# Summing the passing weight quarters on two engines instead of loading them: a Strassen-like matmul on one core

## The chip, the cores and the metric

The kernel runs on one core of a Trainium2 chip. The metric is device time in microseconds, the median of several runs. A core has a matrix engine (TensorE, PE in the profile, with PEld for its loading of stationary operands), three engines for elementwise work (VectorE, DVE; ScalarE, ACT; GpSimd, POOL) and SyncE (SP), which here only issues DMA transfers. Operands lie in SBUF, matmul results in the eight banks of PSUM.

## The reference

```python
B, S, D = 8, 2048, 2048
x = randn(B, S, D)   # float32
w = randn(D, D)      # float32

def reference(x, w):
    cs = np.cumsum(x, axis=1)
    diff = cs - shifted(cs)      # zeros ahead of the first row
    return np.matmul(diff, w)
```

The difference of the running sum is x again, so what is computed is x @ w: 16384 rows by 2048 by 2048, in float32 at the ends. The kernel works with 16-bit operands and scales.

## The kernel before, in words

**Rows.** x is cut into 128 row tiles of 128 rows. The first four (PLAIN = 4) are multiplied plainly in bf16 while the weights arrive. The rest are taken four at a time, tiles g, h = g + 2, g + 1 and h + 1, in 31 groups. The first group is `group_plain`; all others are `group`, and from g = 16 on they take its branch `five` (28 groups).

**Products.** Each group is a block product with fewer multiplications than the plain one: halves of rows and of weights are summed beforehand (S1 to S4 for rows, T1 to T4 for weights), and several of the seven inner products are themselves split once more into seven quarter products. A `product` is 16 matmuls, `steps` are the same in four portions (`go` issues the next), a `quarter` is four matmuls of 128x128 by 128x512 into one bank (L531). In a group of the branch `five` TensorE has 208 matmuls in an order written out by hand. The banks of the quarter products are called q, e, v, w; X and Y are pairs of banks of the larger products.

**Weight quarters.** An `Inner` holds the quarters of one weight half that has been split again: t11, t12, t21, t22 and the sums Q1, Q2, Q3 and Q4 = t21 - Q2 (`fourth`). There are four of them: in_2, in_3, in_4, in_5. Only in_3 has a Q4 of its own place, and in_3.t21 is not kept in place: its place was given to other sums. The four quarters without a place "pass": they use in turn one tile of 128x2048 fp16 in SBUF, `flow` (`passed` is its four parts). Each was written once to DRAM (`keep_flow`, and four transfers for in_3.t21) and is brought back by `bring_flow(i)`, a transfer of 512 KB on SyncE's queue. In a group of the branch `five`, flow holds in turn

- in_2.Q4, for the quarter product `quarter(q, a22, Q.Q4, False)` with Q = in_2 (brought by `bring_flow(0)` at the end of the group before),
- in_3.t21, for `quarter(v, b12, passed, False)` (`bring_flow(3)`),
- in_5.Q4, for `quarter(e, a22, passed, True)` (`bring_flow(1)`),
- in_4.Q4, for `quarter(Y[0], a22, Q.Q4, False)` with Q = in_4 (`bring_flow(2)`).

**Results.** `add` (L542) is a DVE instruction that multiplies a bank by the row tile's unit u and adds it to a running sum C in SBUF; `keep` (L539) is a ScalarE instruction that starts such a sum. `put` sends a finished sum to the output by a DMA on SyncE's queue.

**Row tiles on their way in.** For each tile of a later group, `load` issues two transfers into F on SyncE's queue, `weigh` (L112, ScalarE) takes sums of absolute values of both halves, `scale_of` (L129 to L132, three small DVE instructions) makes m, the scale s = 1/m and the unit u = m x uw, `narrow` (L143, ScalarE) writes the scaled halves as fp16, and `turn` (L156) transposes them by two DMA transfers on SyncE's queue. In `group` the tiles on their way are next_g, next_h, next_k, next_l and `then`.

**Order.** The function `after` chains the instructions of each engine in the order in which the program asks for them, so every engine runs its list in exactly that order, and an instruction that waits holds up all behind it on its engine. This holds for SyncE's queue of transfers too. GpSimd's queue has almost nothing: a reduction over partitions and seven output transfers at the start.

Of the kernel before, what the change touches and what calls it, by code (L numbers as in the profile page):

```python
# [10 lines left out]
def kernel(  # L11
# [6 lines left out]
    nc = tc.nc  # L18
# [12 lines left out]
    ADD = mybir.AluOpType.add  # L31
    SUB = mybir.AluOpType.subtract
    MUL = mybir.AluOpType.mult
# [25 lines left out]
    uw = const.tile([P, 1], f32, name="uw")  # L59
# [16 lines left out]
    def after(engine, ask):  # L76
        if engine in last:
            with tc.issue_after(last[engine].ins):
                said = ask()
        else:  # L80
            said = ask()
        last[engine] = said[-1] if isinstance(said, tuple) else said
        return said
# [37 lines left out]
    def scale_of(t):  # L121
        if t < END:
            m2 = sums_of.pop(t)
            m = small.tile([P, 1], f32, name="m1")
            s = scales[t] = small.tile([P, 1], f32, name="s")
            u = unit[t] = units.tile([P, 1], f32, name="u")
            after(
                "dve",
                lambda: nc.vector.tensor_scalar(m, m2[:, :1], m2[:, 1:], TINY, ADD, MAX),  # L129
            )  # L130
            after("dve", lambda: nc.vector.reciprocal(s, m))  # L131
            after("dve", lambda: nc.vector.tensor_scalar(u, m, uw, None, MUL))  # L132

    def narrowed(t):
        return where[t][0].bitcast(f16)

    def narrow(t, sides=range(2)):
        if t < END:
            s = scales[t]
            for i in sides:  # L140
                after(
                    "act",
                    lambda: nc.scalar.activation(  # L143
                        narrowed(t)[:, ds(i * NH, NH)], where[t][i], COPY, scale=s
                    ),
                )
# [14 lines left out]
    with tc.tile_pool(name="ring", bufs=7) as ring, tc.tile_pool(  # L161
# [97 lines left out]
        def put(c, rows, columns, queue=nc.gpsimd):  # L259
            return queue.dma_start(out2[rows, columns], c)  # L260
# [203 lines left out]
    def one_c():  # L464
        return free.pop(0)
# [23 lines left out]
    passed = [flow[:, k, :] for k in range(4)]  # L489
# [4 lines left out]
    def bring_flow(i):  # L494
        after("sp", lambda: nc.sync.dma_start(flow, spill[i]))

    def less(dst, p, q):
        for k in range(len(dst)):
            after("dve", lambda: nc.vector.tensor_tensor(dst[k], p[k], q[k], SUB))  # L499

    def total(dst, p, q, op):
        after("dve", lambda: nc.vector.tensor_tensor(dst.all, p.all, q.all, op))  # L502

# [24 lines left out]
    def quarter(to, a, b, first):  # L528
        def some():
            for k in range(4):  # L530
                said = nc.tensor.matmul(  # L531
                    to, a[k], b[k], start=(first and k == 0), stop=(k == 3), skip_group_check=True
                )
            return said

        after("pe", some)

    def keep(c, p, u):
        after("act", lambda: nc.scalar.activation(c, p, COPY, scale=u))  # L539

    def add(c, p, u):
        after("dve", lambda: nc.vector.scalar_tensor_tensor(c, p, u, c, MUL, ADD))  # L542
# [5 lines left out]
    def adds(c, p, u):  # L548
        for n in range(2):
            add(c[n], p[n], u)  # L550
# [29 lines left out]
    in_2, in_3 = Inner(B21), Inner(B22)  # L580
    in_3.Q4 = [spare.pop() for _ in range(4)]
    in_4, in_5 = Inner(T4), Inner(T1)
# [113 lines left out]
    def group(g, X, Y, q, e, v, w):  # L696
        h = g + 2
        five = g > PLAIN + 8
# [7 lines left out]
        next_g, next_h, next_k, next_l, then = g + 4, h + 4, g + 5, h + 5, g + 8  # L706
# [3 lines left out]
        def go(some, n=1):  # L710
            for _ in range(n):
                next(some)()
# [72 lines left out]
        quarter(q, a22, Q.Q4, False)  # L785
        add(C11h[0], q, uh)
        put(C11h[0], h, 0)
        if five:
            bring_flow(3)
        total(S4h, A12h, S2h, SUB)  # L790
        one, two, A5 = sums_in(
            S1g, S1h, (*passing[:2], S1h.half(0), passing[3])
# [16 lines left out]
        if five:  # L809
            one()  # L810
            two()
            a11, a12, a22, s1, s2, s3, s4 = A5
            b11, b12, b22, r1, r2, r3, r4 = A3
            N, R = in_5, in_3
            go(P7g)
            quarter(v, a12, N.t21, True)
            C22g, C22h = [one_c()], []
            keep(C22g[0], v, vg)
            quarter(q, a11, N.t11, True)
            one4()  # L820
            add(C22g[0], q, vg)
            add(C12g[0], q, ug)
            weigh(next_k)
            go(P7g)
            quarter(w, b11, R.t11, True)
            add(C12g[0], w, ug)
            quarter(v, b12, passed, False)
            bring_flow(1)
            add(C12g[0], v, ug)
            put(C12g[0], g, 2)  # L830
            turn(next_g, [1])
            go(P7g)
            quarter(e, s1, N.Q1, True)
            C22g += [one_c()]
            C22h = [None, one_c()]
            keep(C22g[1], e, vg)
            keep(C22h[1], e, vh)
            go(P7g)
            two4()
            scale_of(next_k)  # L840
            add(C22g[0], X[0], vg)
            put(C22g[0], g + 1, 2)
            narrow(next_k)
            quarter(q, s2, N.Q2, False)
            add(C22g[1], q, vg)
            add(C12g[1], q, ug)
            quarter(w, r2, R.Q2, False)
            add(C12g[1], w, ug)
            add(C22g[1], X[1], vg)
            go(P7h)  # L850
            quarter(e, r1, R.Q1, False)
            add(C12g[1], e, ug)
            add(C12h[1], e, uh)
            turn(next_k, [0])
            turn(next_h, [0])
            load(next_l, 0)
            go(P7h)
            quarter(v, s4, N.t22, True)
            add(C22g[1], v, vg)
            put(C22g[1], g + 1, 3)  # L860
            load(then, 1)
            quarter(q, s3, N.Q3, False)
            C22h[0] = one_c()
            keep(C22h[0], q, vh)
            add(C22h[1], q, vh)
            add(C12h[1], q, uh)
            go(P7h)
            quarter(e, a22, passed, True)
            bring_flow(2)
            add(C22h[0], e, vh)  # L870
            add(C12h[0], q, uh)
            weigh(next_l)
            quarter(v, r4, R.t22, False)
            add(C12g[1], v, ug)
            put(C12g[1], g, 3)
            go(P7h)
            adds(C22h, Y, vh)
            puts(C22h, h + 1, 1)
            scale_of(next_l)
            quarter(e, b22, R.Q4, False)  # L880
            add(C12h[0], e, uh)
            quarter(w, r3, R.Q3, False)
            add(C12h[0], w, uh)
            put(C12h[0], h, 2)
            add(C12h[1], w, uh)
            put(C12h[1], h, 3)
        else:
            if g == PLAIN + 4:
                in_4.first()
            one()  # L890
            two()
            weigh(next_k)
            seven(A3, in_3, C12g, C12h, P7g)
            turn(next_g, [1])
            turn(next_h, [0])
            scale_of(next_k)
            narrow(next_k)
            if g == PLAIN + 4:
                in_4.fourth()
                keep_flow(2)  # L900
                for k in range(4):
                    after("sp", lambda: nc.sync.dma_start(spill[3][:, k, :], in_3.t21[k]))
                in_4.third()
            else:
                in_5.first()
                in_5.fourth()
                keep_flow(1)
            product((v, w), S1g, T1, True)
            C22g = pair()
            keeps(C22g, (v, w), vg)  # L910
            adds(C12g, (v, w), ug)
            puts(C12g, g, 1)
            load(next_l, 0)
            product((q, e), S1h, T1, True)
            C22h = pair()
            keeps(C22h, (q, e), vh)
            adds(C12h, (q, e), uh)
            puts(C12h, h, 1)
            if g > PLAIN + 4:
                bring_flow(2)  # L920
            go(P7g, 2)
            one4()
            two4()
            turn(next_k, [0])
            adds(C22g, X, vg)
            puts(C22g, g + 1, 1)
            go(P7h, 4)
            adds(C22h, Y, vh)
            puts(C22h, h + 1, 1)
            weigh(next_l)  # L930
            scale_of(next_l)
            load(then, 1)
# [7 lines left out]
        quarter(X[0], a12, Q.t21, False)  # L940
        add(C21g[0], X[0], vg)
        put(C21g[0], g + 1, 0)
        narrow(next_l, [0])
        quarter(e, s1, Q.Q1, True)
        C21h = [None, one_c()]
        keep(C21g[1], e, vg)
        keep(C21h[1], e, vh)
        narrow(next_l, [1])
        quarter(X[1], s4, Q.t22, False)
        turn(next_k, [1])  # L950
        turn(next_l, [0])
# [12 lines left out]
        add(C21h[0], q, vh)  # L964
        put(C21h[0], h + 1, 0)
        if next_g < END:
            bring_flow(0)
        turn(next_l, [1])
        if g == PLAIN + 8:
            in_5.third()  # L970
# [37 lines left out]
```

## Time and profile before

| what | value |
|---|---|
| median of 3 runs | 1531.41 us (1529.73 to 1533.57) |
| the profiled execution | 1542.59 us |
| span of the profiled execution | 1540.8 us |
| granted TensorE clock | 0.996 |
| busy: PE, DVE, ACT, POOL | 1487.4, 1228.7, 912.2, 5.1 us |
| HBM read, written | 210.76 MB, 136.31 MB |
| period of a group of the branch five | 46.06 us |

In the profile, lines such as L542 refer to the program above. A group of instructions is written as tile written <- tiles read. A span is one execution from the first to the last instruction; "idle before" is time in which an engine stood still ahead of an instruction, and the name behind the arrow is what it seems to have waited for. Starts are counted from the start of the span. Matmuls are pipelined: one of 128x512 takes 0.38 us from start to end, while the next starts 0.216 us after it; adds and sums on DVE overlap in the same way to a smaller degree.

### The profile page before, as it was taken

How to read it: one execution, taken by the hardware profiler on the slowest of the kernel's cores; microseconds unless marked ns; L12 is line 12 of the kernel's file. 1: busy time of each engine (PE TensorE's matmuls, PEld its weight loads, DVE VectorE, ACT ScalarE, POOL GpSimd, SP SyncE). 2: the span in 40 equal slices, each digit the busy share in tenths (PEclk: the TensorE clock that was granted, in tenths of full speed). 3: DMA queues.
4: the chain of work that ended last, by engine and by line, in shares of the span. 5: the costliest groups of instructions: out<-in, count | busy, mean ns of one | idle time of the engine just before them, and what ended most of it. 6: DMA issues, size and time to landing. Idle time of an engine off the chain costs nothing.

```text
span 1540.8 us, 20681 instructions
## 1 busy us (share of the span) xinstructions
PE 1487.4 (97%) x6793; PEld 662.5 (43%) x6799; DVE 1228.7 (80%) x2315; ACT 912.2 (59%) x1301; POOL 5.1 (0%) x12
## 2 busy tenths in 40 slices
PE   8988999999999999999999999999999999999998
PEld 3433444444444444444444444444444444444443
DVE  7986777787887778888788877878887788778877
ACT  5866555555656546656556656556656556656542
POOL 0100000000000000000000000000000000000000
PEclk9999999999999999999999999999999999999999
DMA  9988989999999999999999999999999999999984
GB/s 362 354 217 249 225 228 279 280 281 242 278 271 273 281 272 255 283 267 281 276 280 251 292 260 277 272 270 273 283 269 279 277 270 255 280 261 288 274 226 143
DMA packets 395179, 413.49 MB, mean 268 GB/s; under 512 B 276736, under 2 KB 277248, under 8 KB 394944
## 3 DMA queue, kind: packets, MB, share of 16 engines
q1 hardware_dynamic: 394512, 410.35, 95.1%
q0 software_dynamic: 560, 1.84, 0.3%
q8 instruction: 53, 0.87, 0.2%
q14 instruction: 54, 0.44, 0.1%
HBM read 210.76 MB, written 136.31 MB: 225 GB/s over the span
## 4 chain that ended last, share of the span: by engine, by line
PE 56%; DMA 21%; DVE 11%; issue 4%; ACT 4%; SPq 2%; DVEq 0%; ACTq 0%
PE b L531 27%; PE b L512 27%; DMA F<-in_x_dram 7%; DMA flow<-spill 6%; DMA x<-F 6%; DVE c L542 5%; PE b L250 2%; DVE x L502 2%; SPq L156 2%; DVE inner L502 2%; DMA out_dram<-c 2%; ACT F L143 1%; ACT waste L112 1%; ACT c L539 1%; DVE W L499 1%
## 5 line engine op out<-in xcount | busy, mean ns | idle before, releaser
L542 DVE SCALAR_TENSOR_TENSOR c<-b,u,c 128x512 f32<-128x512 f32 x1048 | 744.5, 747 | 179.3 <-PE b L531 108.7
L512 PE MATMUL b<-W,x 128*128 128x512 f16 x3072 | 721.3, 381 | 6.0 <-ACT c L539 4.5
L539 ACT ACTIVATE c<-b,u 128x512 f32<-128x512 f32 x496 | 316.1, 681 | 372.2 <-PE b L512 188.8
L512 PEld LDWEIGHTS <-x 128*128 128x128 f16 x3072 | 301.7, 98 | 373.3 <-issue 12.9
L143 ACT ACTIVATE F<-F,s 128x1024 f16<-128x1024 f32 x246 | 282.1, 1147 | 117.3 <-DVE s L131 114.2
L531 PE MATMUL b<-W,inner 128*128 128x512 f16 x1392 | 338.2, 379 | 13.1 <-DVE c L542 13.1
L112 ACT ACTIVATE waste<-F 128x1024 uint8<-128x1024 f32 x246 | 259.5, 1055 | 107.5 <-DMA F<-in_x_dram 103.6
L531 PEld LDWEIGHTS <-inner 128*128 128x128 f16 x1744 | 170.4, 98 | 223.1 <-issue 20.3
L531 PEld LDWEIGHTS <-x 128*128 128x128 f16 x1560 | 150.3, 98 | 218.1 <-issue 26.7
L531 PE MATMUL b<-W,x 128*128 128x512 f16 x968 | 234.4, 379 | 2.1 <-DVE c L542 0.8
L502 DVE TENSOR_TENSOR x<-x,x 128x1024 f16<-128x1024 f16 (+1 forms) x214 | 120.5, 575 | 7.0 <-PE b L512 2.1
L531 PE MATMUL b<-flow,x 128*128 128x512 f16 x352 | 90.6, 380 | 17.9 <-DVE c L542 9.6
L502 DVE TENSOR_TENSOR inner<-x,x 128x1024 f16<-128x1024 f16 (+1 forms) x122 | 67.9, 556 | 24.6 <-DMA x<-F 24.5
L531 PE MATMUL b<-inner 128*128 128x512 f16 x240 | 61.6, 379 | 0.0
L531 PE MATMUL b<-inner,x 128*128 128x512 f16 x240 | 61.6, 379 | 0.0
L250 PE MATMUL b<-wb,xP 128*128 128x512 bf16 x234 | 56.8, 394 | 3.8 <-DVE xP L222 1.6
L502 DVE TENSOR_TENSOR inner<-x 128x512 f16<-128x512 f16 x60 | 25.2, 421 | 37.4 <-PE b L531 35.7
L129 DVE TENSOR_SCALAR m<-m 128x1 f32<-128x1 f32 x124 | 26.0, 209 | 32.9 <-ACT waste L112 32.7
L112 ACT ACTIVATION_READ_ACCUMULATOR waste<-F 128x1 f32 x246 | 46.5, 189 | 0.0
L502 DVE TENSOR_TENSOR x<-inner,x 128x1024 f16<-128x1024 f16 x62 | 42.6, 687 | 3.2
L502 DVE TENSOR_TENSOR inner<-inner 128x512 f16<-128x512 f16 x112 | 42.4, 421 | 1.0
L237 DVE TENSOR_REDUCE wmax<-W 128x1 f32<-128x1024 f32 x32 | 39.0, 1219 | 3.9 <-DMA W<-in_w_dram 2.4
(53 smaller groups left out, 346.4 us busy)
## 6 DMA issues: line engine op xcount, KB each, us to landing
out_dram<-c SPq DMA_DIRECT2D x496, 256.0 KB, 4.1
F<-in_x_dram SPq DMA_DIRECT2D x246, 512.0 KB, 5.2
flow<-spill SPq DMA_DIRECT2D x114, 512.0 KB, 5.6
W<-in_w_dram SPq DMA_DIRECT2D x32, 512.0 KB, 9.3
W<-in_x_dram SPq DMA_DIRECT2D x16, 256.0 KB, 7.2
x<-F SPq DMA_TRANSPOSE x246, 3.9
out_dram<-o SPq DMA_DIRECT2D x7, 256.0 KB, 3.5
spill<-flow SPq DMA_DIRECT2D x3, 512.0 KB, 2.7
```

Source lines behind the costliest of these rows:

```text
L112: lambda: nc.scalar.activation(waste, where[t][i], ABS, scale=1.0 / ROW, accum_out=sums_of[t][:, i : i + 1],),
L129: lambda: nc.vector.tensor_scalar(m, m2[:, :1], m2[:, 1:], TINY, ADD, MAX),
L143: lambda: nc.scalar.activation(narrowed(t)[:, ds(i * NH, NH)], where[t][i], COPY, scale=s),
L156: lambda: nc.sync.dma_start_transpose(place(t)[i], narrowed(t)[:, ds(i * NH, NH)]),
L237: lambda: nc.vector.tensor_reduce(wmax[:, i : i + 1], wt, AX.X, MAX, apply_absolute_value=True),
L250: lambda: nc.tensor.matmul(ps[r][n], xP[:, r, ko, :], wb[h, ko][:, ds(n * NB, NB)], start=(ko == 0), stop=(ko == KO - 1),),
L499: after("dve", lambda: nc.vector.tensor_tensor(dst[k], p[k], q[k], SUB))
L502: after("dve", lambda: nc.vector.tensor_tensor(dst.all, p.all, q.all, op))
L512: said = nc.tensor.matmul(to[n], a[k], b[k][:, n, :], start=(first and k == 0), stop=(k == KH - 1), skip_group_check=True,)
L531: said = nc.tensor.matmul(to, a[k], b[k], start=(first and k == 0), stop=(k == 3), skip_group_check=True)
L539: after("act", lambda: nc.scalar.activation(c, p, COPY, scale=u))
L542: after("dve", lambda: nc.vector.scalar_tensor_tensor(c, p, u, c, MUL, ADD))
```

## The change

No passing quarter is brought from DRAM in the groups of the branch `five`, and in_2.Q4 is not brought in any group. Each is computed again into flow whenever it is needed: in_2.Q4 and in_3.t21 by four DVE sums each (in_3.t21 as in_3.Q4 + in_3.Q2), in_5.Q4 and in_4.Q4 by four GpSimd sums each, in a new function `pass_fourth`. All have 128x512 fp16 operands in SBUF. Of the loads of flow, only `bring_flow(2)` in the group g = 12 remains. The DVE sums for in_3.t21 stand after the sums of rows for in_3, those for in_2.Q4 at the end of the group, each later in program order than the transfer that they replace or in its place. The GpSimd sums stand where the transfers stood.

Besides, u is computed by GpSimd instead of DVE for all row tiles. In the branch `five`, `scale_of(next_l)` moves behind the last three adds of its stretch on DVE, and in every `group` the first half of `narrow(next_l)` moves behind two `keep` on ScalarE, to the second half.

```diff
@@ scale_of
             after("dve", lambda: nc.vector.reciprocal(s, m))
-            after("dve", lambda: nc.vector.tensor_scalar(u, m, uw, None, MUL))
+            after("pool", lambda: nc.gpsimd.tensor_scalar(u, m, uw, None, MUL))
@@ new function
+    def pass_fourth(i):
+        for k in range(4):
+            after("pool", lambda: nc.gpsimd.tensor_tensor(passed[k], i.t21[k], i.Q2[k], SUB))
@@ group
         put(C11h[0], h, 0)
-        if five:
-            bring_flow(3)
         total(S4h, A12h, S2h, SUB)
...
         if five:
             one()
             two()
+            for k in range(4):
+                after('dve', lambda: nc.vector.tensor_tensor(passed[k], in_3.Q4[k], in_3.Q2[k], ADD))
             a11, a12, a22, s1, s2, s3, s4 = A5
...
             quarter(v, b12, passed, False)
-            bring_flow(1)
+            pass_fourth(in_5)
             add(C12g[0], v, ug)
...
             quarter(e, a22, passed, True)
-            bring_flow(2)
+            pass_fourth(in_4)
             add(C22h[0], e, vh)
             add(C12h[0], q, uh)
             weigh(next_l)
...
             puts(C22h, h + 1, 1)
-            scale_of(next_l)
             quarter(e, b22, R.Q4, False)
             add(C12h[0], e, uh)
             quarter(w, r3, R.Q3, False)
             add(C12h[0], w, uh)
             put(C12h[0], h, 2)
             add(C12h[1], w, uh)
             put(C12h[1], h, 3)
+            scale_of(next_l)
...
         put(C21g[0], g + 1, 0)
-        narrow(next_l, [0])
         quarter(e, s1, Q.Q1, True)
         C21h = [None, one_c()]
         keep(C21g[1], e, vg)
         keep(C21h[1], e, vh)
-        narrow(next_l, [1])
+        narrow(next_l)
...
         if next_g < END:
-            bring_flow(0)
+            less(passed, in_2.t21, in_2.Q2)
         turn(next_l, [1])
```

## The prediction, made before the changed kernel had run

> **What bounds the kernel now.** The page came first. TensorE is busy nearly the whole span at a full clock, so only the gaps between its matmuls can be won; the rows say whose they are.
>
> ```profile
> PE 1487.4 (97%) x6793; PEld 662.5 (43%) x6799; DVE 1228.7 (80%) x2315; ACT 912.2 (59%) x1301; POOL 5.1 (0%) x12
> PE 56%; DMA 21%; DVE 11%; issue 4%; ACT 4%; SPq 2%; DVEq 0%; ACTq 0%
> F<-in_x_dram SPq DMA_DIRECT2D x246, 512.0 KB, 5.2
> flow<-spill SPq DMA_DIRECT2D x114, 512.0 KB, 5.6
> x<-F SPq DMA_TRANSPOSE x246, 3.9
> ```
>
> The chain that ended last runs through DMA for 21%. The waits of the steady part, 290 to 1495 us, name the partners:
>
> ```profile
> PEld L531 <- DMA flow<-spill: 19.0, 24, 2.0
> DVE inner L502 <- DMA x<-F: 16.5, 23, 1.5
> PE b L531 <- DVE c L542: 16.4, 28, 1.9
> ```
>
> To size them I read the timeline of TensorE alone. From 655.77 to 662.67 us 32 matmuls start, 0.216 us each; a quarter product (four) takes 0.863. A group of four row tiles has 52 such steps, 44.9 us, and repeats every 46.06. I number the steps 0 to 51 from the group's first product. Wherever a piece starts later than the one before it plus its count times 0.216, the difference is lost time:
>
> ```profile
> 646.68 3.62 PE L531 MATMUL b<-W,x 128*128 128x512 f16 x16
> 651.25 2.75 PE L531 MATMUL b<-W,inner 128*128 128x512 f16 x12 [0.94 <-DVE c L542]
> ...
> 679.08 1.03 PE L531 MATMUL b<-W,x 128*128 128x512 f16 x4
> 680.18 1.04 PE L531 MATMUL b<-flow,x 128*128 128x512 f16 x4
> ```
>
> Step 47 was due at 646.68 + 16 x 0.216 = 650.14 and came at 651.25: 1.11 lost. Step 28 was due at 679.94: 0.24 lost. Added up over 290 to 1495 us (26 groups), the steps that read flow (18 and 28) lose 16.7 us, step 47 loses 16.2, step 51 loses 5.9 (0.21 a time, one running add after step 49; the change leaves it). Little else is lost.
>
> Step 47 rewrites bank e, which DVE must have read. That read stood behind the weighing of the last tile:
>
> ```profile
> 644.15 4.70 DVE L542 SCALAR_TENSOR_TENSOR c<-b,u,c 128x512 f32<-128x512 f32 x7 [0.83 <-ACT c L539]
> 650.01 0.21 DVE L129 TENSOR_SCALAR m<-m 128x1 f32<-128x1 f32 x1 [1.16 <-ACT waste L112]
> 650.26 0.16 DVE L131 RECIPROCAL s<-m 128x1 f32<-128x1 f32 x1
> 650.34 0.20 DVE L132 TENSOR_SCALAR u<-m,uw 128x1 f32<-128x1 f32 x1
> 650.45 2.91 DVE L542 SCALAR_TENSOR_TENSOR c<-b,u,c 128x512 f32<-128x512 f32 x4
> ```
>
> Step 18 is a wait on DVE, which waits for a transpose issued right behind a flow load; step 28 waits for its own flow load. From the chain of waits, 880 to 930 us:
>
> ```profile
> 890.57 8.20 DMA x<-F
> ...
> 901.24 0.67 DVE c L542
> 901.92 0.04 issue
> 901.96 1.04 PE b L531 x4
> ...
> 905.31 6.19 DMA flow<-spill
> 911.50 0.05 issue
> 911.54 1.04 PE b L531 x4
> ```
>
> SyncE issued flow at 890.02 and the transpose at 890.57. It landed after 8.20 us, against a median of 3.9.
>
> **The change part by part.** *Flow loads.* 113 of 114 go (28 groups with three, 29 with the one at the end; one remains at g = 12): 59 of 211 MB read, and three to four issues a group on SyncE's queue, each 0.38 us. Transposes and loads behind them move up. Gained: the 16.7 us of steps 18 and 28, if the new producers are in time.
>
> *Last scale later.* add(C12h[0], e) moves ahead of m, s and u: 1.16 of wait and 0.44 of work leave the way to step 47. The seven adds end at 648.85, e is read by 649.6, before 650.14. Gained: 16.2 us. What is late next: narrow(next_l) now follows three adds (3 x 0.67) and both keeps of e on ScalarE. Its halves end about 0.8 us before and 0.4 after the next group's start, against 4.2 and 1.2 before it now. SyncE reaches these transposes 0.6 before and 4.8 us after that start (655.16, 660.55), so nearly all is covered; without that cover DVE's sum at 667.86 would be late. keep(C21h[0]) on ScalarE slips about 1 us behind the narrowing, and its reader is DVE's last add, reached then anyway.
>
> *Two quarters on DVE.* Eight sums a group; 128x512 f16 sums start 0.335 us apart (658.18, 658.52, 658.85), so 1.34 us for four. The four for in_2 follow the last add (657.8) and push the next seven sums; DVE then sat 2.41 us idle before 663.81, which hides them. The four for in_3 follow the sum at 676.73, end at 678.4 and fill a wait of 1.26 before 678.41; step 28 needs them at 679.94. Zero on the path; without either cover, 1.34 x 28 = 38 us. No queue gets longer than its idle time: DVE gains 2.7 us a group, loses four u (0.11 each), and had over 7 us of waits.
>
> *Two quarters on GpSimd.* No row shows a sum there. Nearest below: the same sum on DVE, 0.42. Nearest above: the slowest work per element, the 128x128 scan on DVE, 0.425, times four: 1.70. I take 1.70, the cautious end, since GpSimd's known rows (memset 128x1, 0.10) say nothing per element. Time allowed: for in_4 from the end of step 40 (645.12) to step 50 (653.83 less the 1.11 lost, plus 0.65 for the fourth matmul), 8.25 us or 2.06 a sum; for in_5 from 680.97 to 690.96, 2.5 a sum. Either bound fits: zero. Behind a waiting sum on that queue stand only u, which are read most of a group later. The u themselves: 0.10 (that memset) to 0.20 (the DVE row), off the path.
>
> *What the two engines do to each other.* No row has both working in SBUF. GpSimd's first batch begins as step 28 ends and meets the two sums of two4:
>
> ```profile
> 682.67 0.41 DVE L502 TENSOR_TENSOR x<-x,x 128x512 f16<-128x512 f16 x1
> 683.00 0.42 DVE L502 TENSOR_TENSOR inner<-x,inner 128x512 f16<-128x512 f16 x1
> ...
> 684.77 5.00 DVE L542 SCALAR_TENSOR_TENSOR c<-b,u,c 128x512 f32<-128x512 f32 x7 [0.26 <-PE b L531]
> ```
>
> DVE has room behind them: waits of 0.26 and 0.83, one u less (0.11), and 0.57 that the read of e then has to spare: 1.8 us. Lower bound of the cost: nothing. If each sum waits for one GpSimd sum of 1.70, two4 ends about 1.6 late: covered. Upper bound: two4 waits for all four sums, 4 x T - 1.46 late, so 4T - 3.26 beyond cover: 3.5 us a group at 1.70. I take 0.1 to 0.2 us a group, 4 us in all, because most margins become thin.
>
> The Trainium skill speaks against this pairing: by its page "SBUF — State Buffer", section "Who interferes with whom", a VectorE instruction with two SBUF inputs and a GpSimd instruction that reads SBUF exclude each other, and the later one blocks for the whole of the other. No row before shows it; by it two4 loses one or two GpSimd sums and the running adds (one input in PSUM) nothing. "GPSIMD Engine Reference", section 3.1, measures 4497 ns for 2048 elements, an estimate of 1.1 us for 512; by that figure both batches end with some 3 us to spare.
>
> **The sum**, against the profiled execution's own 1542.59 us (span 1540.8): 16.7 + 16.2, and some 3 of the 4.6 that the same steps lose between 200 and 290 us (1.61, 2.5, 0.46), less 4: 32 saved, 1510.6. The median of the runs is 1531.41, 11.2 below. If that difference lies elsewhere, 32 come off: 1499. If it lies wholly in these waits, 21: 1510. I take 27: **1504 us**; own range 1494 to 1513.
>
> **Rivals.**
>
> *Held sums (slower).* two4 waits for GpSimd's whole batch. For: the batch starts 1.5 us before two4 in each group. Against: nothing shows that a batch is kept together. It turns the gain into a loss from T = 1.10 on, where 28 x (4T - 3.26) passes 32; at 1.70 it costs 98, net 66: 1597; at 1.2, 43, net 11: 1542. Chance 0.15.
>
> *GpSimd slow (slower).* Over 2.06 us a sum, step 50 waits; at 2.5, 4 x 0.44 x 28 = 49 less 32: 1548. For: nothing about its speed is known from rows. Against: it would be over five times DVE's time. Chance 0.09.
>
> *Transfers stay late.* Landing times hold although flow is gone, because narrow(next_l) comes later; step 18 still waits for DVE. Steps 28 and 47 alone: about 19 saved, 1513 to 1518. For: 16.5 us of DVE waits on transposes. Against: the 8.20 us stood behind a flow load. Chance 0.14.
>
> *Gains and losses cancel*, within 0.3% (about 5 us, what a measurement of this kernel can tell from no change): 1527 to 1536, chance 0.06. That flow traffic would remain has no place: the loads are gone from the queue.
>
> **How the numbers follow.** The main case has 0.56. It and late transfers make it faster by over 0.3%: 0.70, with 0.01 from held sums of a short T: 0.71. Within: 0.06. Slower: 0.23. The range, 1491 to 1537, leaves out a little below and most of the two slower rivals.
>
> **What would show it.** Right: no wait of TensorE on flow at steps 18 and 28 or on DVE at step 47, a period near 45.2 us with 0.21 left at step 51, F loads landing under 5.2 us, GpSimd sums under 2.06. Wrong: steps 37 to 47 waiting for DVE adds while the sums of two4 start after GpSimd's last one; step 50 waiting for GpSimd; or step 18 waiting with its transpose still near 8 us.

## The result, and the profile after

| | before | after |
|---|---|---|
| median, us | 1531.06 (1529.73 to 1533.57, 4 runs) | 1508.07 (1507.42 to 1509.20, 4 runs) |
| ratio, 95% interval | | 0.9849 [0.9832, 0.9866] |
| the profiled execution, us | 1542.59 | 1509.20 |
| span of it, us | 1540.8 | 1507.4 |
| HBM read, MB | 210.76 | 151.52 |
| period of a group of the branch five, us (mean of the last 26) | 46.40 (45.2 to 48.3) | 45.38 (45.37 to 45.39) |

The changed kernel is faster by 23.0 us between the medians and by 33.4 us between the profiled executions. The profiled execution before, 1542.59 us, is not among the four runs of its median and stands 9 us above the slowest of them. The 46.06 us given above as the period before is that of one group, 701.79 to 747.85 us; the mean is 46.40. In later comparisons on two other chips the kernel before took medians of 1541.7 us, on a third 1538.5 with runs from 1531.6 to 1544.9; the changed kernel stayed between 1507.4 and 1511.7 in all its runs. The time of the kernel before moves from chip to chip and from run to run, that of the kernel after hardly does. Side by side on one chip the ratio was 0.9799 [0.9783, 0.9816], 32.2 us.

From the page of the kernel after, its parts 1, 4 and 6 (four lines added to the program move L502 to L506, L512 to L516, L531 to L535, L539 to L543 and L542 to L546):

```profile
PE 1480.5 (98%) x6799; PEld 661.8 (44%) x6799; DVE 1329.6 (88%) x2419; ACT 914.2 (61%) x1301; POOL 328.9 (22%) x360
...
PE 75%; DVE 13%; issue 4%; DMA 4%; ACT 3%; SPq 0%; DVEq 0%; ACTq 0%
...
F<-in_x_dram SPq DMA_DIRECT2D x246, 512.0 KB, 4.9
...
x<-F SPq DMA_TRANSPOSE x246, 3.4
```

DMA had 21% of the chain that ended last and has 4%. Transposes land in 3.4 us instead of 3.9, loads of rows in 4.9 instead of 5.2. DVE's busy share rose from 80% to 88%, more than its 228 new sums of 0.335 us (76 us, 5 points of 1507) explain; the rest is sums that take longer, shown below. From the list of waits of the kernel after, 290 to 1465 us (engine and line, what it waited for, us in total, times, longest):

```profile
POOL flow L503 <- PE b L535: 248.8, 52, 5.1
...
DVE c L546 <- PE b L535: 66.4, 79, 1.1
PEld L535 <- DVE c L546: 14.8, 26, 0.6
...
DVE inner L506 <- DMA x<-F: 0.2, 1, 0.2
```

No wait on flow by TensorE is left, DVE's waits on transposes went from 16.5 to 0.2 us, and one new regular wait has appeared: 26 times, once in each group, TensorE's weight loads wait for a running add. The timeline of TensorE shows where (start, length, operation):

```profile
664.33 1.03 PE L535 MATMUL b<-flow,x 128*128 128x512 f16 x4
...
672.10 1.89 PE L535 MATMUL b<-W,inner 128*128 128x512 f16 x8
673.82 1.03 PE L516 MATMUL b<-W,x 128*128 128x512 f16 x4
674.94 1.04 PE L535 MATMUL b<-flow,inner 128*128 128x512 f16 x4
...
677.57 3.61 PE L535 MATMUL b<-W,x 128*128 128x512 f16 x16
681.01 2.75 PE L535 MATMUL b<-W,inner 128*128 128x512 f16 x12
```

Step 47, 1.11 us late in the group shown before, is on time: due at 677.57 + 16 x 0.216 = 681.03, it came at 681.01.

The product that reads in_5.Q4 was due at 673.82 + 0.863 = 674.68 and came at 674.94. It does not wait for flow: GpSimd had been ready for 5 us. It rewrites bank e and waits for an add that DVE is late with. This is step 40, and it loses 0.24 us in every group. DVE and GpSimd in the same group of the kernel after, from their timelines:

```profile
664.79 4.69 POOL L503 TENSOR_TENSOR flow<-W 128x512 f16<-128x512 f16 x4 [4.43 <-PE b L535]
```

```profile
667.06 1.41 DVE L506 TENSOR_TENSOR x<-x,x 128x512 f16<-128x512 f16 x1
668.39 1.37 DVE L506 TENSOR_TENSOR inner<-x,inner 128x512 f16<-128x512 f16 x1
...
670.00 12.32 DVE L546 SCALAR_TENSOR_TENSOR c<-b,u,c 128x512 f32<-128x512 f32 x18
```

The two sums of two4 (the last sums of rows for in_4) took 0.41 and 0.42 us before; beside GpSimd's batch they take 1.41 and 1.37. After them 18 adds follow without a pause, so DVE has no time left to catch up.

To compare kernels, the lost time of TensorE from 290 us to the end, added up by step from its timeline as in the prediction (us; a dash is nothing over 0.1 at a time):

| kernel | 18 and 28 | 40 | 43 | 47 | 50 | 51 | sum |
|---|---|---|---|---|---|---|---|
| before | 16.7 | - | - | 16.2 | - | 6.1 | 39.1 |
| after | - | 6.3 | - | - | - | 5.8 | 12.1 |
| e1_late_scale_only | 12.8 | - | - | - | - | 5.8 | 18.6 |
| e2_flow_only | - | 6.3 | - | 29.7 | - | 6.1 | 42.1 |
| e3_u_on_dve | - | 9.4 | - | - | - | 5.7 | 15.1 |
| e4_two4_late | - | - | - | - | - | 5.8 | 5.8 |
| e5_all_on_dve | - | - | 25.3 | - | - | 5.8 | 31.1 |
| e6_gpsimd_double | - | - | - | - | 18.4 | - | 18.4 |
| e7_only_in2 | 2.3 | - | - | 23.2 | - | 5.8 | 31.3 |
| e8_two4_late_s2_first | - | - | - | - | - | - | 0.3 |
| e9_flow_only_two4_late | - | - | - | 10.0 | - | 6.1 | 16.1 |

The 0.3 us of e8_two4_late_s2_first fall at step 48, in one group. For the part before 290 us the start of the second group of the branch five (g = 20) is compared: 283.4 us before, 277.1 after, 275.5 to 280.3 in the others.

### The profile page after: what moved, and what is told of

It is laid out like the page before. It is cut to its first block, busy times and chain, and to the rows that moved or that the text cites. A ratio compares the mean times of both kernels' runs of the same rounds, so it can differ in the third digit from the quotient of the medians.

```text
span 1507.4 us, 21215 instructions
## 1 busy us (share of the span) xinstructions
PE 1480.5 (98%) x6799; PEld 661.8 (44%) x6799; DVE 1329.6 (88%) x2419; ACT 914.2 (61%) x1301; POOL 328.9 (22%) x360
## 3 DMA queue, kind: packets, MB, share of 16 engines
HBM read 151.52 MB, written 136.31 MB: 191 GB/s over the span
## 4 chain that ended last, share of the span: by engine, by line
PE 75%; DVE 13%; issue 4%; DMA 4%; ACT 3%; SPq 0%; DVEq 0%; ACTq 0%
PE b L535 37%; PE b L516 36%; DVE c L546 9%; DVE inner L506 3%; DMA W<-in_w_dram 2%; PE b L250 2%; ACT c L543 1%; DMA x<-F 1%; DVE W L499 1%; DMA W<-in_x_dram 0%; DMA out_dram<-c 0%; DVE x L506 0%; ACT W L361 0%; ACT waste L112 0%; DVE m L129 0%
## 5 line engine op out<-in xcount | busy, mean ns | idle before, releaser
L546 DVE SCALAR_TENSOR_TENSOR c<-b,u,c 128x512 f32<-128x512 f32 x1048 | 736.6, 745 | 125.4 <-PE b L535 81.3
L516 PE MATMUL b<-W,x 128*128 128x512 f16 x3072 | 717.9, 380 | 5.9 <-ACT c L543 3.8
L543 ACT ACTIVATE c<-b,u 128x512 f32<-128x512 f32 x496 | 315.5, 680 | 283.6 <-issue 147.8
L516 PEld LDWEIGHTS <-x 128*128 128x128 f16 x3072 | 300.9, 98 | 370.5 <-issue 8.4
L535 PE MATMUL b<-W,inner 128*128 128x512 f16 x1392 | 338.3, 379 | 0.0
L535 PEld LDWEIGHTS <-inner 128*128 128x128 f16 x1744 | 168.5, 98 | 215.3 <-DVE c L546 15.3
L132 POOL TENSOR_SCALAR u<-m,uw 128x1 f32<-128x1 f32 x124 | 66.6, 542 | 817.0 <-DVE m L129 809.0
L535 PEld LDWEIGHTS <-x 128*128 128x128 f16 x1560 | 152.1, 98 | 195.9 <-issue 14.6
L535 PE MATMUL b<-W,x 128*128 128x512 f16 x968 | 234.2, 379 | 1.5
L503 POOL TENSOR_TENSOR flow<-W 128x512 f16<-128x512 f16 x140 | 163.6, 1195 | 291.2 <-PE b L535 286.8
L506 DVE TENSOR_TENSOR x<-x,x 128x1024 f16<-128x1024 f16 (+1 forms) x214 | 147.2, 700 | 6.2 <-PE b L516 1.1
L503 POOL TENSOR_TENSOR flow<-W,W 128x512 f16<-128x512 f16 x84 | 94.9, 1160 | 0.0
L535 PE MATMUL b<-flow,x 128*128 128x512 f16 x352 | 90.3, 379 | 2.5 <-DVE c L546 2.5
L506 DVE TENSOR_TENSOR inner<-x,x 128x1024 f16<-128x1024 f16 (+1 forms) x122 | 67.4, 553 | 3.3 <-DMA x<-F 3.3
L535 PE MATMUL b<-inner,x 128*128 128x512 f16 x240 | 61.6, 379 | 0.7 <-DVE x L506 0.7
L535 PE MATMUL b<-inner 128*128 128x512 f16 x240 | 61.6, 379 | 0.4 <-DVE c L546 0.4
L506 DVE TENSOR_TENSOR inner<-x,inner 128x512 f16<-128x512 f16 x60 | 51.7, 862 | 0.0
L506 DVE TENSOR_TENSOR x<-inner,x 128x1024 f16<-128x1024 f16 x62 | 42.4, 683 | 3.2
```

The costliest lines, as they stand in the source:

```text
L132: after("pool", lambda: nc.gpsimd.tensor_scalar(u, m, uw, None, MUL))
L503: after("pool", lambda: nc.gpsimd.tensor_tensor(passed[k], i.t21[k], i.Q2[k], SUB))
L516: said = nc.tensor.matmul(to[n], a[k], b[k][:, n, :], start=(first and k == 0), stop=(k == KH - 1), skip_group_check=True,)
L535: said = nc.tensor.matmul(to, a[k], b[k], start=(first and k == 0), stop=(k == 3), skip_group_check=True)
```

## The experiments

The kernels were compared in three sets, each on one chip with the kernel before beside it: e1 to e4; e5, e6, e9 and the changed kernel again; e7, e8 and e4 again.

**The changed kernel again**, beside the second set.

> The changed kernel itself, to stand beside the others on one chip. If the time of the kernel before differs between chips through its transfers and that of the changed kernel does not, it stays at 1506 to 1510 us wherever the kernel before stands; if the chips differ in everything alike, it moves with the kernel before (1518 beside 1542).

Measured: 1509.48 us beside 1541.73 of the kernel before, ratio 0.9799 [0.9783, 0.9816]. It stayed where it was while the kernel before stood 10.7 us higher. Why the kernel before varies between chips and between runs was not settled. Within one execution the profiles show that its groups take 45.2 to 48.3 us each, and those of the changed kernel 45.37 to 45.39; that the same waits make the runs differ is not shown.

**Only the late scale** (e1_late_scale_only), the kernel before with

```diff
             puts(C22h, h + 1, 1)
-            scale_of(next_l)
             quarter(e, b22, R.Q4, False)
...
             put(C12h[1], h, 3)
+            scale_of(next_l)
...
-        narrow(next_l, [0])
...
-        narrow(next_l, [1])
+        narrow(next_l)
```

> The kernel before with only the last scale moved behind the three adds, and the narrowing with it; all four loads of flow stay, u stays on DVE. Theory A (step 47 waits because the read of bank e stands behind the scale on DVE): the gaps at step 47, 16.2 us of the 33 in the profile before, go, and those at steps 18 and 28 stay near 17 us; of the 23 us that the whole change brought, about half: 1519 to 1523 us. Rival B (the loads of flow make everything late, step 47 included): nothing moves, 1529 to 1533. Rival C (TensorE runs ahead and meets flow later): step 47 is clean and steps 18 and 28 grow by what it gave up, 1526 to 1531.

Measured: 1519.42 us, ratio 0.9853 [0.9833, 0.9873], beside 1541.76: 22 us of some 32. Step 47 is clean and steps 18 and 28 keep 12.8 of their 16.7 us. Theory A holds, and rivals B and C fall. The waits of this kernel, 290 to 1475 us, show what is left:

```profile
PEld L531 <- DMA flow<-spill: 16.0, 22, 2.3
...
DVE inner L502 <- DMA x<-F: 11.5, 18, 1.4
```

**Only flow and u** (e2_flow_only), the changed kernel with the reverse of the diff above.

> The changed kernel with the last scale and the narrowing put back to their old places: flow is computed, u is on GpSimd. Theory A: no gaps at steps 18 and 28, but step 47 still waits for DVE, 0.4 to 0.7 us a group: 1516 to 1524 us. Rival B (fewer transfers let the last load land early enough): step 47 is clean too, 1507 to 1511.

Measured: 1540.22 us, ratio 0.9994 [0.9979, 1.0008]: nothing gained at all. Both theories missed. Steps 18 and 28 are clean as theory A said, but step 47 rose from 16.2 to 29.7 us, 1.14 a group instead of 0.62. The chain of waits of this kernel, in order of time:

```profile
679.33 0.88 PE b L535 x4
680.21 0.80 SPq L156
681.00 0.05 issue
681.07 0.03 issue
681.10 5.08 DMA F<-in_x_dram
686.23 0.94 issue
687.17 0.20 ACT waste L112
...
688.64 0.22 DVE m L129
688.89 0.16 DVE s L131
689.05 0.66 DVE c L546
689.71 0.04 issue
689.75 2.77 PE b L535 x12
```

The last load of rows is issued at 681.10, 33.9 us after the first product of its group (647.22); before, it was 32.8 (688.57 less 655.77) in the group shown, and 33.4 on average over 26 groups against 33.9 here. It stands on SyncE's queue behind two transposes, and the first of these waits for the narrowing of next_k, whose scale stands on DVE behind two4. That gave theory G.

**Flow and u, with two4 out of GpSimd's way** (e9_flow_only_two4_late), e2 with

```diff
-            two4()
             scale_of(next_k)
...
             add(C22g[1], v, vg)
             put(C22g[1], g + 1, 3)
+            two4()
             load(then, 1)
```

> Flow computed and the last scale at its old place, as in e2_flow_only, with the two sums of two4 moved behind the next eight adds. Theory G (in e2 the held sums of two4 made the scale of next_k late, with it its narrowing, the transposes on SyncE's queue and the load of the last tile behind them, about 1.0 us, and so step 47 waited 1.14 us a group): step 47 waits 0.1 to 0.4 us a group, 1511 to 1520 us. Rival H (step 47 waits more only because TensorE reaches it earlier, the load is as late as ever): step 47 waits about 1 us, only step 40's 0.24 goes, 1531 to 1536 us.

Measured: 1512.79 us, ratio 0.9821 [0.9803, 0.9839]. Moving two DVE sums of 0.42 us gave 27 us (on another chip than e2; the kernel before took 1541.8 and 1541.7 us on the two). In the table above 19.7 of them are step 47's and 6.3 step 40's. Step 47 waits 0.39 us a group (10.0 over 26). SyncE's queue, first e2_flow_only, then this kernel:

```profile
678.35 2.65 SPq L156 DMA_TRANSPOSE x<-F  x2
681.10 0.53 SPq L100 DMA_DIRECT2D F<-in_x_dram  x1
```

```profile
668.49 3.03 SPq L156 DMA_TRANSPOSE x<-F  x2
671.62 0.53 SPq L100 DMA_DIRECT2D F<-in_x_dram  x1
```

Counted from the first products of their groups (647.22 and 639.02), the load is issued at 33.9 in e2 and at 32.6 here, 1.3 us earlier; the means over 26 groups are 33.90 and 32.65. The edit also takes two4's own time, 0.75 us, out of the way of that scale. In e7 below, where two4 stands in its old place, GpSimd has no sums and three loads of flow are still in the queue, the mean is 32.87, so some 1.0 of the 1.25 us comes from the sums being held. Theory G holds, rival H falls.

**u on DVE** (e3_u_on_dve), the changed kernel with

```diff
-            after("pool", lambda: nc.gpsimd.tensor_scalar(u, m, uw, None, MUL))
+            after("dve", lambda: nc.vector.tensor_scalar(u, m, uw, None, MUL))
```

> The changed kernel with u on DVE again. Theory A (u is 0.11 us of DVE, of which only the one ahead of the adds before step 40 is uncovered): step 40 waits 0.35 instead of 0.24 us, 28 x 0.11 = 3 us more: 1508 to 1512 us. Rival D (DVE is so full in these groups that each u counts, 4 x 0.11 x 28 = 12 us): 1518 to 1522.

Measured: 1514.83 us, ratio 0.9818 [0.9799, 0.9837]. Step 40 waits 0.36 us a group (9.4 over 26), as theory A had it (0.35). The time is 2.8 us above its range; of the 6.1 us between the profiles of this kernel and of the changed one, 3.0 lie before 290 us (the group g = 20 begins at 280.2 us, at 277.1 and 277.0 in the two profiles of the changed kernel), and their cause is open. Rival D falls: only the u ahead of step 40 counts in the groups.

**two4 late** (e4_two4_late), the changed kernel with the diff of e9.

> The changed kernel with the two sums of two4 moved behind the eight adds that follow them on DVE, away from GpSimd's first batch. Theory E (DVE sums with two operands in SBUF wait for GpSimd's sum, 0.42 becomes 1.4 us, and this makes step 40 late by 0.24): the two sums take 0.42 again, step 40 is on time, 27 x 0.24 = 6.5 us less than the changed kernel: 1500 to 1504 us. Rival F (DVE is full from there to step 47 whatever the order): the gap moves to steps 43 to 47 and the time stays at 1507 to 1510.

Measured: 1501.15 us, ratio 0.9728 [0.9708, 0.9747]. DVE and GpSimd in this kernel:

```profile
672.06 0.41 DVE L506 TENSOR_TENSOR x<-x,x 128x512 f16<-128x512 f16 x1
672.39 0.42 DVE L506 TENSOR_TENSOR inner<-x,inner 128x512 f16<-128x512 f16 x1
```

```profile
663.03 4.50 POOL L503 TENSOR_TENSOR flow<-W 128x512 f16<-128x512 f16 x4 [4.42 <-PE b L535]
```

The batch is over at 667.53, the sums take their old time and step 40 loses nothing. GpSimd's batch is shorter too, 4.50 against 4.69. Theory E holds, rival F falls.

**Everything on DVE** (e5_all_on_dve), the changed kernel with

```diff
-            after("pool", lambda: nc.gpsimd.tensor_tensor(passed[k], i.t21[k], i.Q2[k], SUB))
+            after("dve", lambda: nc.vector.tensor_tensor(passed[k], i.t21[k], i.Q2[k], SUB))
```

> The changed kernel with the sums for in_5.Q4 and in_4.Q4 on DVE, in the same places of the program; GpSimd makes only u. Theory A (GpSimd is needed because DVE has no room between step 28 and step 47): step 40 is nearly on time, since four sums take 1.34 us where the held ones lost 1.95, but the four after step 40 hold up the adds before steps 43 and 47: 1.0 to 1.4 us a group lost there, 1530 to 1545 us. Rival (mutual exclusion costs as much as the sums themselves): 1504 to 1510 us.

Measured: 1526.41 us, ratio 0.9907 [0.9891, 0.9923], 17 us above the changed kernel beside it and 4 us below the range of theory A. The mechanism is the one named: step 40 is on time, step 43 loses 0.93 us a group. The rival falls. DVE in this kernel:

```profile
677.59 6.96 DVE L546 SCALAR_TENSOR_TENSOR c<-b,u,c 128x512 f32<-128x512 f32 x10
684.47 0.41 DVE L503 TENSOR_TENSOR flow<-W 128x512 f16<-128x512 f16 x1
684.80 1.09 DVE L503 TENSOR_TENSOR flow<-W,W 128x512 f16<-128x512 f16 x3
685.80 4.89 DVE L546 SCALAR_TENSOR_TENSOR c<-b,u,c 128x512 f32<-128x512 f32 x7
```

The adds before step 43 stand behind four sums. GpSimd is slower at this work but has the time.

**GpSimd's sums twice** (e6_gpsimd_double), the changed kernel with

```diff
         for k in range(4):
-            after("pool", lambda: nc.gpsimd.tensor_tensor(passed[k], i.t21[k], i.Q2[k], SUB))
+            for _ in range(2):
+                after("pool", lambda: nc.gpsimd.tensor_tensor(passed[k], i.t21[k], i.Q2[k], SUB))
```

> The changed kernel with each GpSimd sum of flow made twice (same result). Theory A (a batch of 4.5 us lies in a window of about 8.8 us before step 50): a batch of 9.3 us ends 0.5 us late for the last of the four sums, step 50 waits some 0.5 us a group, step 40 and two4 as before (each DVE sum meets one GpSimd sum): 1518 to 1526 us. Rival K (DVE sums are held for as long as GpSimd has sums in its queue): two4 ends 4 to 5 us later, 3 us a group more: 1580 and above. Rival L (GpSimd has slack beyond that): 1506 to 1512 us.

Measured: 1514.71 us, ratio 0.9831 [0.9813, 0.9849]. Step 50 waits 0.68 us a group, near the 0.5 of theory A, but the time is 3 us below its range, since the waits of steps 40 and 51 went. Why step 40 went shows in GpSimd's and DVE's timelines of this kernel:

```profile
668.54 9.70 POOL L504 TENSOR_TENSOR flow<-W 128x512 f16<-128x512 f16 x8 [4.42 <-PE b L536]
```

The second of the eight alone:

```profile
669.78 1.16 POOL L504 TENSOR_TENSOR flow<-W 128x512 f16<-128x512 f16 x1
```

```profile
670.81 0.41 DVE L507 TENSOR_TENSOR x<-x,x 128x512 f16<-128x512 f16 x1
671.14 1.38 DVE L507 TENSOR_TENSOR inner<-x,inner 128x512 f16<-128x512 f16 x1
```

GpSimd's second sum ends at 669.78 + 1.16 = 670.94: the first DVE sum began 0.13 us before that seam and took its old 0.41, and only the second was held. With one sum held instead of two, DVE is 1 us late and step 40 is in time, with two4 in its old place: it is the holding, and not the order on DVE alone, that costs step 40 its 0.24 us. Rival L falls too: step 50 waits, and the time lies 3 us above its range. Rival K falls: a batch of eight holds a DVE sum no longer than one of four.

**Only in_2.Q4 by DVE** (e7_only_in2), the kernel before with

```diff
         if next_g < END:
-            bring_flow(0)
+            less(passed, in_2.t21, in_2.Q2)
         turn(next_l, [1])
```

> The kernel before with only the load of in_2.Q4 at the end of the group replaced by four DVE sums; three loads of flow and the early scale stay. Theory A (step 18 waits because the last transpose stood behind that load): the DVE waits on transposes, 16.5 us in the steady part before, fall under 3, and step 18 is on time; step 28 keeps its waits, and step 47 takes back what step 18 gave: 1528 to 1540 us beside 1542. Rival (the transposes are late because ScalarE narrows late or DMA is full): waits on transposes stay above 10 us.

Measured: 1526.14 us, ratio 0.9921 [0.9894, 0.9948], beside 1538.47: 12 us, 2 us below the range. DVE's waits on transposes are gone from its list of waits, 290 to 1495 us, which ends with

```profile
PE b L531 <- DVE c L542: 19.3, 24, 2.6
PEld L531 <- DMA flow<-spill: 6.4, 13, 0.8
PE b L531 <- DMA flow<-spill: 1.1, 4, 0.3
```

Theory A holds for step 18, and the rival falls. Steps 18 and 28 together fall from 16.7 to 2.3 us, all of it at step 28, so most of step 28's waits go too, which theory A did not have. The flow loads land after 4.9 us (median) instead of 5.6; that this is the reason is not shown. Step 47 rises from 16.2 to 23.2, as theory A had it: half of what the steps 18 and 28 gave up is taken back there, without any sum on GpSimd.

**two4 late and s2 first** (e8_two4_late_s2_first), beside e4_two4_late again:

```diff
-        quarter(X[1], s4, Q.t22, False)
-        turn(next_k, [1])
-        turn(next_l, [0])
         quarter(q, s2, Q.Q2, False)
         add(C21g[1], q, vg)
+        quarter(X[1], s4, Q.t22, False)
+        turn(next_k, [1])
+        turn(next_l, [0])
```

> e4_two4_late once more, to stand beside the next kernel on one chip: 1499 to 1503 us.

> e4_two4_late with the quarter products s2 (step 49) and s4 (step 48) exchanged, so that two steps instead of one lie between the product s2 and the product s3 that continues its bank after one add. Theory: the 0.21 us that step 51 waits in each of 30 groups go, 6 us: 1493 to 1497 us. Rival: the product s2 now waits at step 48 for the keep of its bank on ScalarE, which the weighing holds up (it ended 0.7 us before that step in the changed kernel), so that a part comes back: 1498 to 1503 us.

Measured: 1502.30 us, ratio 0.9762 [0.9738, 0.9787], for e4_two4_late and 1496.40 us, ratio 0.9725 [0.9701, 0.9749], for this one, beside 1538.47. Step 51's 0.21 us are gone, and from 290 us on TensorE loses 0.3 us in all, once, at step 48, where the rival had put its wait. This is the fastest version tried, 13 us under the changed kernel on another chip (1509.48).

## Why the prediction was right, and where it was off

*Flow loads, 16.7 us at steps 18 and 28.* They went, and the transposes behind the flow load with them (0.2 us of waits left). As a term of its own it depends on the others. With the late scale left out it is worth nothing (e2, ratio 0.9994): GpSimd's sums hold two4, step 40 then loses 6.3 us, and step 47 loses 13.5 more than before. With two4 out of GpSimd's way it is worth 29 us alone (e9). The waits are also in part in series, as e7 shows, where 14.4 us less at steps 18 and 28 bring 7.0 more at step 47. Alone the two parts give 29 us (e9, two4 late) and 22 (e1), together with two4 late 40.6 (e4), less than their sum.

*Last scale, 16.2 us at step 47.* Right in place and in size. Alone it gives 22 us (e1): 16.2 at step 47, 3.9 at steps 18 and 28, and some 3 before 290 us. It also covers the lateness of the last load that the held sums cause (19.7 us at step 47 between e2 and e9), which the prediction didn't see: it named two4's delay, but not that scale_of(next_k), its narrowing and the load of next_l stand behind it.

*Before 290 us*, 3 us were forecast and the two profiles differ by 6.2 (283.4 against 277.1); other kernels' profiles spread over 4.9 us there, so little follows.

*Two quarters on DVE at zero.* Right: no step waits for them.

*GpSimd's sums at 1.70 us, inside windows of 2.06 and 2.5.* They take 1.16 us, between the bounds 0.42 and 1.70, and step 50 never waits; with twice the work it waits 0.68. A batch begins 0.46 us after the start of the step that reads flow (664.79 against 664.33), and not as that step ends, so it ran 2.27 us ahead of two4 and not 1.46. The page "GPSIMD Engine Reference" of the Trainium skill, section 3.1, from whose 4497 ns the prediction estimated 1.1 us, agrees, though that figure is for fp32 and these sums are fp16.

*What the two engines do to each other, 4 us.* This term was mis-sized. The sums of two4 wait for one GpSimd sum each and end 1.95 us late (669.76 instead of 667.06 + 0.33 + 0.42 = 667.81), against 1.6. The cover of 1.8 us was reckoned to step 47, and its largest part, the wait of 0.83 (the row at 644.15), stands behind the add that step 40 needs: step 40 of that group had begun at 644.09. Step 40, which rewrites bank e after that add, comes first; its cover was 1.7 us (1.95 less the 0.24 lost). It loses 0.24 us in each group, 6.3 us from 290 us on. The Trainium skill's rule ("SBUF — State Buffer", section "Who interferes with whom") is what the traces show: two inputs in SBUF wait (0.42 becomes 1.4), adds with one input in PSUM do not (0.745 us on average, 0.747 before; the 281 that ran mostly beside a GpSimd sum for flow took 0.743).

*The sum.* For a profiled execution 1510.6 us were forecast, 1509.2 came. That this is so close is partly luck: the held sums cost over 2 us more than forecast, and the part before 290 us gave 3 more. For the median 1504 were forecast, 1508.07 came. The choice between 21 and 32 us of gain was set at 27; the first comparison gave 23.0, because there the kernel before stood at its lower times, and 32.2 came on the chip of the second. Of the 11.2 us between profile and median 1.1 were left in the changed kernel (1509.20 against 1508.07).

*Rivals.* Held sums are real, but are held one by one, not for a batch (e6), so their price stayed under the gain: 6.3 us here. Without the late scale it was 26 us (e2 against e9) and took the whole gain, which the prediction did not have. GpSimd was fast enough. Transfers did not stay late. The period is 45.38 us against 45.2 forecast, the difference being step 40.

## What to carry to other kernels

Waits along one loop are not a sum: take one away and the next in the loop may take part of its time, so find which instruction the later wait hangs on, and whether an edit moves that too. When GpSimd gets sums in SBUF, look at which two-operand DVE sums fall into the same stretch and move those, not the GpSimd work; a delayed small sum costs what stands behind it on its queue, here a scale, a narrowing, a transpose and a load. And when a read is late, reckon the room to the first bank that is rewritten, not to the one that waited before.

## What the runs showed of the hardware that was not expected

A DVE sum held by GpSimd lost about 1 us each time, while the batch of four GpSimd sums that met two of them lost 0.19 us in all (4.69 against 4.50). The small u on GpSimd is held in its turn: 0.28 us where DVE runs adds, 0.84 in the kernel after where DVE runs a 128x1024 sum at the same time (653.87 and 653.89), which itself keeps its 0.67 us.
